# Two transformer layers on one core: four PSUM pairs in the V, K and Q stage, V's low parts dealt out otherwise, h's range in the third head, the last output half in another bank

## Chip, core and metric

One NeuronCore of a Trainium2 chip. The metric is the device time of one execution in microseconds (us). The five engines are named as in the profile: PE (TensorE, matrix products), DVE (VectorE), ACT (ScalarE), POOL (GpSimd) and SP (SyncE, which here only issues DMAs). PSUM, into which PE writes, has eight banks of 128 x 512 fp32; a "pair" is two neighbouring banks, 128 x 1024.

## What is computed

DEPTH is 2: layer 0 is multi-head latent attention, layer 1 differential attention, over 1024 latent tokens and 256 context tokens, width 1024. Cut to what matters here:

```python
for i in range(DEPTH):
    shift, scale, gate = adaln(c, ada_w[i], ada_b[i])          # also for the context
    h = x * (1 + scale) + shift;  h_c = ctx * (1 + scale_c) + shift_c
    if i == 0: o, o_c = mla_mixer(h, h_c, ...)                 # 16 heads, 96-wide q and k, 64-wide v
    else:      o, o_c = diff_mixer(h, h_c, ...)                # 8 heads, two softmaxes each
    x = layer_norm(ALPHA * x + gate * (o @ out_w[i]), ln_g[i], ln_b[i])
    # context the same, in layer 0 only
# mla_mixer: q from a 256-wide and k, v from a 128-wide latent; o = softmax(q k^T * s) v, times silu(gate)
```

## The kernel before, in words

Every fp32 operand is held as a high and a low part, and a product takes three matmuls (`mm3`, L185 to L187). The program runs in stages: projections of layer 0; a short stage that makes V for all heads and K and Q of head 0 (L873 to L884); the 16 heads of layer 0; its output projection (L1146 to L1180); layer 1.

PE's order is written out by hand in all stages that matter here (`manual_schedule`, engine P; in the V, K and Q stage DVE's order too, in the output projection all four engines'). Elsewhere a planner orders DVE, ACT, POOL and SP, and it also chooses, among the buffers of a tag, the one that comes free first. Every engine runs its own instructions in order.

**V, K and Q stage.** Five generators are stepped through in a fixed list (L880). Each makes a product in a PSUM pair (`pair()`), and the pair comes free when its last reader is done. In PE's order, with names that the text below uses:

- P: the rotary part of q (12 matmuls of 512 columns); DVE shuffles and multiplies it (L290, L291), then L294 and L295 work on SBUF alone.
- K, Q: k and q of two heads; ACT writes the high part (stkH, stqH, L181), DVE the low part (stkL, stqL, L182). Kc, Pc, Qc are the same for the context, 256 columns.
- V0 to V9: V of a tile of 128 tokens, all heads (6 matmuls). ACT writes the high part Vh (L650). The low part Vl goes one of two ways: on DVE (L656), one instruction that reads the pair; or ACT copies the pair into a buffer `op` (L653) and POOL subtracts (L654). `op` has one buffer, so a second ACT copy waits until POOL has read the first.
- M0 to M3, MC: row maxima of head 0's first 512 queries: scores (L757, L763), DVE's maximum (L759, L764, L765), a turn on PE (L768) and a write into a row of qH (L769). The first true scores wait for it. M0 reads q and k that went through DMAs (L86) from the staging tiles, KH among them.

**A head** has 11 units; a unit makes scores for 256 keys (L833 to L835), ACT's exponential (L777) and rounding (L778), POOL's low part (L779), and two units later the products with V (L845 to L848). S0 is head 0's first unit. Between the units stand the row maxima for later queries and, in head 0 only, `h1_range` (L544 to L565): 4 small matmuls (L552) and 16 small DVE instructions that bound the size of the next layer's input. Its results are read only in layer 1.

**Output projection.** For each of 8 tiles two halves, y0 in a bank of tag `a` and y1 in the only bank of tag `b`. Behind tile 7 all eight banks become tag `b`, one is taken and left unused (L1181), and the first product of layer 1 (its K) takes another.

```python
    set_banks(a=3, d=2)                 # 613: three pairs, and two banks for the heads' results
            if t % 2 == 0:              # 651: which tiles of V go by ACT and POOL
            y1, y0 = bank("b"), bank("a")   # 1146
        bank("b")                       # 1181
```

## Time and profile before

| | |
|---|---|
| three runs | 1799.22, 1794.52, 1797.15 us; median 1797.15 |
| the profiled execution's own time | 1797.62 us |
| its span in the trace | 1795.8 us (1.8 us lie outside it) |
| mean granted PE clock | 0.988 of full speed |
| PE, DVE, ACT, POOL busy | 93%, 69%, 62%, 44% of the span |
| V, K and Q stage | 221.2 to 257.6 us in the span |
| heads 0 to 15 | 257.6 us to about 767 us |
| output projection of layer 0, with the changed tile 7 | to 905 us |

How rows are read: in a timeline a row has start, duration (us), engine, line of the kernel, operation, output<-inputs, shapes, number of instructions, and in brackets the engine's idle time before it and what ended that. A row of PE lists a matmul's whole passage; two matmuls overlap, so the pace is the distance of the starts. A row of the stretches has the length, then each engine's busy time and, behind "PEclk", the granted clock.

### The profile page before, as it was taken

How to read it: one execution, taken by the hardware profiler on the slowest of the kernel's cores; microseconds unless marked ns; L12 is line 12 of the kernel's file. 1: busy time of each engine (PE TensorE's matmuls, PEld its weight loads, DVE VectorE, ACT ScalarE, POOL GpSimd, SP SyncE). 2: the span in 40 equal slices, each digit the busy share in tenths (PEclk: the TensorE clock that was granted, in tenths of full speed). 3: DMA queues.
4: the chain of work that ended last, by engine and by line, in shares of the span. 5: the costliest groups of instructions: out<-in, count | busy, mean ns of one | idle time of the engine just before them, and what ended most of it. 6: DMA issues, size and time to landing. Idle time of an engine off the chain costs nothing. (4 is left out here: it accounts for less than half of the span.)

```text
span 1795.8 us, 36757 instructions
## 1 busy us (share of the span) xinstructions
PE 1668.3 (93%) x14564; PEld 1237.5 (69%) x14564; DVE 1236.9 (69%) x2047; ACT 1117.9 (62%) x2233; POOL 796.3 (44%) x722
## 2 busy tenths in 40 slices
PE   7999989999999998999999999989999999986998
PEld 7999955656666565577866666767676757574876
DVE  7658566566665757557746777787778777979564
ACT  3541167877777787835536676767675766666442
POOL 1422136767776676845541222222314131435454
PEclk9999999999999999999999999999999999998999
DMA  8258520110111112164432213121212122223331
GB/s 304 80 156 256 164 56 23 44 44 21 42 46 34 43 44 81 51 217 161 148 117 74 58 54 79 55 78 54 68 41 64 35 68 58 62 61 124 101 116 70
DMA packets 111225, 154.84 MB, mean 86 GB/s; under 512 B 13415, under 2 KB 84679, under 8 KB 111054
## 3 DMA queue, kind: packets, MB, share of 16 engines
q1 hardware_dynamic: 102654, 144.90, 27.3%
q10 hardware_dynamic: 8400, 7.61, 1.3%
q8 instruction: 114, 1.87, 0.4%
q14 instruction: 57, 0.47, 0.1%
HBM read 98.65 MB, written 27.07 MB: 70 GB/s over the span
## 5 line engine op out<-in xcount | busy, mean ns | idle before, releaser
L779 POOL TENSOR_TENSOR pl<-p,ph 128x1024 f16<-128x1024 f32 (+1 forms) x176 | 364.1, 2074 | 149.3 <-ACT ph L778 122.6
L1361 ACT ACTIVATE p<-ps_b,mx 128x512 f32<-128x512 f32 (+1 forms) x384 | 230.3, 617 | 89.0 <-DVE mx L1357 84.9
L777 ACT ACTIVATE p<-ps_a,esc 128x1024 f32<-128x1024 f32 (+1 forms) x176 | 189.0, 1074 | 93.4 <-PE ps_a L835 87.5
L759 DVE TENSOR_REDUCE mx<-ps_a 128x1 f32<-128x1024 f32 x128 | 155.2, 1222 | 127.7 <-PE ps_a L757 127.7
L778 ACT CAST ph<-p 128x1024 f16<-128x1024 f32 (+1 forms) x176 | 177.1, 1006 | 5.5
L1355 DVE TENSOR_REDUCE mx<-ps_b 128x1 f32<-128x512 f32 x256 | 165.3, 679 | 0.0
L848 PE MATMUL ps_d<-Vh,pl 128*128 128x65 f16 x1344 | 146.0, 194 | 4.5 <-POOL pl L779 4.4
L845 PE MATMUL ps_d<-Vh,ph 128*128 128x65 f16 x1344 | 148.2, 195 | 0.0
L847 PE MATMUL ps_d<-Vl,ph 128*128 128x64 f16 x1344 | 146.9, 193 | 0.0
L1386 POOL TENSOR_TENSOR sm<-sm,us 128x1 f32<-128x1 f32 x64 | 17.9, 280 | 273.6 <-DVE sm L1365 263.5
L1338 PE MATMUL ps_b<-KS,QS 128*128 128x512 f16 (+1 forms) x384 | 125.7, 345 | 12.9 <-DVE pl L182 7.1
L845 PEld LDWEIGHTS <-ph 128*128 128x128 f16 x1344 | 123.3, 97 | 18.0 <-issue 4.6
L847 PEld LDWEIGHTS <-ph 128*128 128x128 f16 x1344 | 123.9, 98 | 12.1
L833 PE MATMUL ps_a<-qH,KH 100*128 100x512 f16 x320 | 121.5, 380 | 8.5 <-ACT p L777 4.2
L1339 PE MATMUL ps_b<-KS,Q 128*128 128x512 f16 (+1 forms) x384 | 129.0, 345 | 0.0
L848 PEld LDWEIGHTS <-pl 128*128 128x128 f16 x1344 | 123.2, 97 | 5.8 <-POOL pl L779 5.8
L181 ACT ACTIVATE ph<-ps_b,lcf 128x512 f16<-128x512 f32 (+1 forms) x192 | 115.1, 647 | 19.3 <-PE ps_b L1374 19.3
L182 DVE SCALAR_TENSOR_TENSOR pl<-ps_b,lcf,ph 128x512 f16<-128x512 f32 (+1 forms) x192 | 117.1, 653 | 13.5 <-ACT ph L181 13.5
L1374 PE MATMUL ps_b<-idr,p 128*128 128x128 f32 x640 | 103.6, 278 | 22.8 <-ACT p L1361 14.7
L834 PE MATMUL ps_a<-qH,KL 96*128 96x512 f16 x320 | 121.3, 379 | 0.0
L835 PE MATMUL ps_a<-qL,KH 96*128 96x512 f16 x320 | 120.7, 377 | 0.0
L1384 PE MATMUL ps_b<-vh,pl 128*128 128x128 f16 x640 | 111.3, 220 | 5.3 <-DVE pl L182 5.3
(427 smaller groups left out, 5261.0 us busy)
## 6 DMA issues: line engine op xcount, KB each, us to landing
ws<-in_dw SPq DMA_DIRECT2D x28, 512.0 KB, 3.9
adw<-in_ada_w SPq DMA_DIRECT2D x24, 512.0 KB, 4.9
adaw<-in_ada_w SPq DMA_DIRECT2D x16, 512.0 KB, 7.4
g<-sg_d SPq DMA_DIRECT2D x16, 512.0 KB, 7.3
sg_d<-gg ACTq DMA_DIRECT2D x40, 128.0 KB, 3.7
o_d<-op SPq DMA_DIRECT2D x7, 640.0 KB, 3.9
xt<-in_xT SPq DMA_DIRECT2D x16, 256.0 KB, 4.4
wgs<-in_w_in SPq DMA_DIRECT2D x32, 128.0 KB, 3.3
```

The source lines that it names most:

```text
L759: dve.tensor_reduce(mx[:, t, 0:1], ps, axis=AX.X, op=ALU.max)
L777: act.activation(p32[:, :n], st, AF.Exp, scale=esc0)
L778: act.copy(ph[:, :n], p32[:, :n])
L779: pool.tensor_tensor(pl[:, :n], p32[:, :n], ph[:, :n], op=ALU.subtract)
L833: pe.matmul(s_, kh[:nr, ks], QH[:nr, :], start=True, stop=False)
L845: pe.matmul(pv[:, t, :], ph[:, ts], Vh[:, k, h, :], start=(k == kcs[0] and t == 0), stop=False, skip_group_check=True)
L847: pe.matmul(pv[:, t, :V0], ph[:, ts], Vl[:, k, h, :], start=False, stop=False, skip_group_check=True)
L848: pe.matmul(pv[:, t, :], pl[:, ts], Vh[:, k, h, :], start=False, stop=(k == NT - 1), skip_group_check=True)
L1338: pe.matmul(out, qs[m][:, ts], ks[m][:, c0:c0 + n], start=True, stop=False)
L1339: pe.matmul(out, q1[m][:, ts], ks[m][:, c0:c0 + n], start=False, stop=True)
L1355: dve.tensor_reduce(mx[:, 2 + 2 * m + i:3 + 2 * m + i], b, axis=AX.X, op=ALU.max, negate=True)
L1361: act.activation(p[m][:, c0:c0 + n], b, AF.Exp, bias=nb, accum_out=sm[:, 2 + 3 * m + i:3 + 3 * m + i])
```

## The change

1. The V, K and Q stage gets four pairs instead of three and two single banks; the cut into three pairs and two banks follows behind it.
2. V0, V2, V4, V6 and V9 get their low parts on DVE; V1, V3, V5, V7 and V8 by ACT and POOL (before: the odd tiles on DVE, the even ones by ACT and POOL).
3. MC moves ahead of V7.
4. `ab1_of` and `h1_range` are asked for in head 2 instead of head 0.
5. y1 of tile 7 goes to the bank of tag `e`, and no bank is taken unused before layer 1's first product.

```diff
@@ -610 @@
-    set_banks(a=3, d=2)
+    set_banks(a=4)
@@ -648 prod_v0 @@
-            if t % 2 == 0:
+            if t in (1, 3, 5, 7, 8):
@@ -879 @@
         for g in (pq, pk, pq, vg, pq, pq, vg, pk, pk, pq, pq1, vg, pq2, pq2, pq2, vg,
-                  pm, vg, pm, vg, pm, vg, pm, vg, pm, vg, pm, vg):
+                  pm, vg, pm, vg, pm, vg, pm, pm, vg, vg, pm, vg):
             next(g)
+    set_banks(a=3, d=2)
@@ -948 @@
-            if h == 0:
+            if h == 2:
                 ab1_of()
-            hr = [(h1_range(pair), (0, 1, 0, 1, 1))] if h == 0 else []
+            hr = [(h1_range(pair), (0, 1, 0, 1, 1))] if h == 2 else []
@@ -1143 @@
-            y1, y0 = bank("b"), bank("a")
+            y1, y0 = bank("b" if t < 7 else "e"), bank("a")
@@ -1178 @@
         set_banks(b=8)
-        bank("b")
```

What the built programs show of the order. DVE in the V, K and Q stage, before, from P's last two steps on (the number behind a tile's name is its buffer; ps_a_2599 is Q's pair, ps_a_2616 V1's):

```order
L294 TENSOR_TENSOR rsw_2536<-rsw_2536,cs_2549 128x1024
L295 TENSOR_TENSOR rr_2537<-rr_2537,rsw_2536 128x1024
L182 SCALAR_TENSOR_TENSOR stqL_2541<-ps_a_2599,qsc_70,stqH_2540 128x1024
L182 SCALAR_TENSOR_TENSOR stpL_2543<-rr_2537,qsc_70,stpH_2542 128x1024
L656 SCALAR_TENSOR_TENSOR Vl<-ps_a_2616,vsc_68,Vh 128x1024
L182 SCALAR_TENSOR_TENSOR stkL_2539<-ps_a_2625,ksc_69,stkH_2538 128x256
```

The same place now (ps_a_2589 is V0's pair, ps_a_2598 Q's, ps_a_2643 V2's):

```order
L295 TENSOR_TENSOR rr_2537<-rr_2537,rsw_2536 128x1024
L656 SCALAR_TENSOR_TENSOR Vl<-ps_a_2589,vsc_68,Vh 128x1024
L182 SCALAR_TENSOR_TENSOR stqL_2541<-ps_a_2598,qsc_70,stqH_2540 128x1024
L182 SCALAR_TENSOR_TENSOR stpL_2543<-rr_2537,qsc_70,stpH_2542 128x1024
L182 SCALAR_TENSOR_TENSOR stkL_2539<-ps_a_2625,ksc_69,stkH_2538 128x256
L656 SCALAR_TENSOR_TENSOR Vl<-ps_a_2643,vsc_68,Vh 128x1024
```

The low part of V0 now stands on DVE ahead of Q's, and that of V1 has left it.

ACT at the end of the stage, now, from V6's high part to head 0's first exponential (ps_a_2737 is V7's pair, ps_a_2748 V8's, ps_a_2762 V9's):

```order
L650 ACTIVATE Vh<-ps_a_2717,vsc_68 128x16x64
L650 ACTIVATE Vh<-ps_a_2737,vsc_68 128x16x64
L653 ACTIVATE op_2745<-ps_a_2737,vsc_68 128x1024
L650 ACTIVATE Vh<-ps_a_2748,vsc_68 128x16x64
L653 ACTIVATE op_2756<-ps_a_2748,vsc_68 128x1024
L650 ACTIVATE Vh<-ps_a_2762,vsc_68 128x16x64
L777 ACTIVATE p_341_2548<-ps_a_2778,esc_71 128x1024
```

Before, the copies into `op` were V6's and V8's, with V7's high part alone between them; now those of V7 and V8 follow each other.

DVE in head 2 now, at the maxima of its second half of queries:

```order
L553 TENSOR_REDUCE hm<-ps_a_3937 128x2
L764 TENSOR_REDUCE mx_3794<-ps_a_3944 128x4
L555 TENSOR_SCALAR hm<-hm 128x1
L769 SCALAR_TENSOR_TENSOR qcH_3676<-ps_a_3963,sh_72,selt_64 2x256
L556 TENSOR_TENSOR hm<-hm 128x1
L557 SCALAR_TENSOR_TENSOR hm<-hm 128x1
L765 TENSOR_REDUCE ng_3795<-mx_3794 128x4
L300 TENSOR_SCALAR hm<-hm 128x1
L301 RECIPROCAL hm<-hm 128x1
L303 TENSOR_SCALAR hun<-hm 128x1
L302 TENSOR_SCALAR hsc<-hm 128x1
L560 TENSOR_TENSOR hm<-hm,hsc 128x1
```

These rows, and six more up to L769's write into qH, stood at the same place of head 0 before, row for row; in head 0 now only L764, L769, L765 and L769 are left there. The instructions of `ab1_of` and the first reductions of `h1_range` (L538 to L547) have not moved on DVE: the planner puts them into the stage before V, K and Q in both programs.

## The prediction

> **What bounds the kernel now.** I read the totals first, then PE's waits in the changed stage, then the stretches, then the rows behind each wait.

> ```profile
> PE 1668.3 (93%) x14564; PEld 1237.5 (69%) x14564; DVE 1236.9 (69%) x2047; ACT 1117.9 (62%) x2233; POOL 796.3 (44%) x722
> ```

> PE is busy for 93% of the span. So in most stages nothing but PE's own pace counts, and time can only be won where PE stands idle or runs at a low clock. PE's waits from 221 us to 258 us, the V, K and Q stage (matrix product and what it waited for: us in total, times, longest):

> ```profile
> PE ps_a L768 <- DVE ng L765: 2.1, 1, 2.1
> PE ps_a L185 <- DVE stqL L182: 2.0, 1, 2.0
> PE ps_a L757 <- DVE Vl L656: 1.3, 2, 0.7
> PE ps_a L185 <- DVE mx L759: 1.1, 2, 0.5
> PE ps_a L185 <- DVE Vl L656: 0.6, 1, 0.6
> ```

> That is 7.1 us of waiting, all of it for DVE. The stretches (length, then busy us of PE, PEld, DVE, ACT, POOL, the granted clock, DMA share, GB/s) show a second loss:

> ```profile
> 221.20:257.60 36.40, 29.23 (x121) 21.08 (x120) 23.23 (x22) 21.50 (x23) 11.68 (x7) 0.91 0.30 80
> 234.80:241.60 6.80, 6.17 (x21) 4.55 (x20) 2.42 (x4) 3.14 (x6) 2.06 (x1) 0.50 0.38 92
> ```

> From 234.80 to 241.60 PE ran at half clock. Its 6.17 busy us there would be 3.1 at full clock, so the spell costs 3.1 us. No engine fills the stage: the fullest behind PE, DVE, is busy for 23.23 of 36.40 us. It is bound by hand-overs, that is by which reader releases which pair.

> **The change part by part.** All sums are made against the profiled execution, 1797.62 us, 0.47 us above the median of the three runs, 1797.15.

> **Term 1, the stage.** The rows of the first long wait, from the timeline (start, duration):

> ```profile
> 227.95 1.22 DVE L294 TENSOR_TENSOR rsw<-rsw,cs 128x1024 f32<-128x1024 f32 x1
> ...
> 229.10 2.07 POOL L654 TENSOR_TENSOR Vl<-op,Vh 128x1024 f16<-128x1024 f32 x1 [5.58 <-ACT op L653]
> 229.20 3.06 DVE L295 TENSOR_TENSOR rr<-rr,rsw 128x1024 f32<-128x1024 f32 x1
> ...
> 232.18 1.27 DVE L182 SCALAR_TENSOR_TENSOR stqL<-ps_a,qsc,stqH 128x1024 f16<-128x1024 f32 x1
> ...
> 233.51 0.50 PE L185 MATMUL ps_a<-wvH,latH 128*128 128x512 f32 x1 [2.04 <-DVE stqL L182]
> ```

> L295 has the shape of L294, yet it takes 3.06 us instead of 1.22, and it does so while POOL's 2.07 us instruction runs beside it. Now V0's low part is DVE's, so POOL has nothing at that point. I take L294's 1.22 for L295 (the other end is 3.06, if POOL wasn't the cause), so it ends at 230.4 instead of 232.2. V0's low part (1.28) follows, to 231.65. With four pairs V2 uses V0's pair, no longer Q's, and starts at 231.7 instead of 233.51. [...]

> For the rest of the stage I need the pace of PE and of the readers. Two starts on PE, the readers' groups (times, busy, mean ns) and one transfer:

> ```profile
> 223.99 0.39 PE L185 MATMUL ps_a<-latH,wkH 128*128 128x512 f32 x1
> ...
> 225.35 0.39 PE L185 MATMUL ps_a<-wvH,latH 128*128 128x512 f32 x1
> ```

> ```profile
> L654 POOL TENSOR_TENSOR Vl<-op,Vh 128x1024 f16<-128x1024 f32 x5 | 10.3, 2068 | 24.4 <-ACT op L653 24.4
> L650 ACT ACTIVATE Vh<-ps_a,vsc 128x1024 f16<-128x1024 f32 x9 | 10.0, 1114 | 7.8 <-PE ps_a L187 7.8
> ...
> L653 ACT ACTIVATE op<-ps_a,vsc 128x1024 f32<-128x1024 f32 x5 | 5.5, 1107 | 0.0
> L656 DVE SCALAR_TENSOR_TENSOR Vl<-ps_a,vsc,Vh 128x1024 f16<-128x1024 f32 x4 | 5.1, 1281 | 5.9 <-ACT Vh L650 5.9
> L759 DVE TENSOR_REDUCE mx<-ps_a 128x1 f32<-128x1024 f32 x4 | 4.7, 1213 | 0.0
> ```

> ```profile
> KH<-stkH SPq DMA_DIRECT2D x16, 160.0 KB, 2.6
> ```

> Six matmuls of 512 columns take 225.35 - 223.99 = 1.36 us; six of 256 half of that, 0.7; a maximum's two score products a third, 0.45. The new order, walked with these and 0.05 to 0.15 us for each hand-over:

> - V2 runs 231.7 to 233.1. Pc takes V1's pair, which ACT frees: Q's high part to 230.9, V1's to 232.1, P's to 233.2, the copy into `op` to 234.2. Pc starts at 234.25 (before 236.01), and Qc and V3 follow to 237.05.
> - M0 needs Kc's part of KH. ACT writes it by 234.65, and 2.6 us later it has landed: M0 at 237.5. This is the new wait where the pairs no longer stop PE: 0.45 us.
> - M0 to M3, MC and V4 to V8 are 5 x 0.45 + 5 x 1.36 = 9.05 us of PE. Waits of 0.4 (V6 for V4's low part), 0.1 (V7 for M2's maximum) and 0.3 (V8 for V6's low part) are left: V8 ends at 247.4.
> - DVE then ends M3's maximum, L764 and L765 at 248.5; L768 at 248.65; V9 1.36; S0 at 250.05.

> The same places before, PE's and ACT's:

> ```profile
> 254.53 1.22 DVE L764 TENSOR_REDUCE mx<-ps_a 128x4 f32<-128x1024 f32 x1
> ...
> 256.08 0.22 PE L768 MATMUL ps_a<-idr,ng 128*4 128x128 f32 x1 [2.12 <-DVE ng L765]
> ...
> 257.58 0.39 PE L833 MATMUL ps_a<-qH,KH 100*128 100x512 f16 x1
> ...
> 259.10 1.11 ACT L777 ACTIVATE p<-ps_a,esc 128x1024 f32<-128x1024 f32 x1 [0.20 <-PE ps_a L835]
> ...
> 261.76 1.11 ACT L777 ACTIVATE p<-ps_a,esc 128x1024 f32<-128x1024 f32 x1 [0.47 <-PE ps_a L835]
> ```

> S0 comes 257.58 - 250.05 = 7.5 us earlier: 4.4 of waits that shrink and 3.1 for the spell, which I take as gone, since the wait of 2.04 us just before it is gone. Not all of that lasts. `op` has one buffer, and V7's and V8's copies now stand next to each other: POOL works on V7's from 248.2 to 250.25, V8's copy waits for that and ends at 251.4, V9's high part at 252.45, and only then comes the first exponential: 6.65 before 259.10. It keeps ACT busy until the second (1.11, then L778's rounding of 1.05) at 254.7, which is 7.06 before 261.76. From there PE leads again. **Term 1: -7.1 us.** Bounds: with L295 at 3.06 the first 1.8 us go; if V8's copy hides, 0.5 to 1.0 more is won; KH landing late costs up to 1.2; the spell's return 3.1.

> **Term 2, `h1_range` out of head 0, and term 3, into head 2.** The same stretch (fourth unit's scores to the sixth's) in head 2, then in head 0:

> ```profile
> 330.56:335.65 5.09, 4.96 (x72) 3.21 (x69) 4.01 (x6) 3.82 (x4) 3.73 (x3) 1.00 0.32 103
> 265.82:274.05 8.23, 5.41 (x76) 3.80 (x73) 7.41 (x21) 5.12 (x5) 5.95 (x4) 1.00 0.09 24
> ```

> With `h1_range` the stretch takes 3.14 us more, though its matmuls are 5.41 - 4.96 = 0.45. The rest lies here:

> ```profile
> 269.65 2.12 POOL L779 TENSOR_TENSOR pl<-p,ph 128x1024 f16<-128x1024 f32 x1 [0.83 <-ACT ph L778]
> ...
> 270.03 1.76 DVE L556 TENSOR_TENSOR hm<-hm 128x1 f32<-128x1 f32 x1
> ...
> 272.08 0.22 PE L768 MATMUL ps_a<-idr,ng 128*4 128x128 f32 x1 [1.44 <-DVE hm L300]
> ...
> 334.45 2.13 POOL L779 TENSOR_TENSOR pl<-p,ph 128x1024 f16<-128x1024 f32 x1 [0.77 <-ACT ph L778]
> ```

> L556 has one column, yet it takes 1.76 us, until POOL's L779 ends; L765 stands behind it, PE's L768 waits 1.44 for that, and the next scores behind qH's row wait 1.4 more. The rows in the order of the program stand in head 2 just as they stood in head 0, and L779 starts there at the same distance from the unit (3.89 us behind the fourth unit's scores in head 2, 3.83 in head 0). So I take the collision over whole: -3.14 and +3.14, **sum 0**. Bounds of the sum: -3.1, if head 2 covers it all, to +3.1, if the two gaps bring a half-clock spell.

> **Term 4, the last output half.** PE, DVE and ACT there:

> ```profile
> 904.71 0.68 DVE L1083 TENSOR_TENSOR z<-ps_b,gate 128x512 f32<-128x512 f32 x1
> ...
> 905.44 0.38 PE L185 MATMUL ps_b<-h1H,wx 128*128 128x512 f16 x1 [2.00 <-DVE z L1083]
> ...
> 908.40 1.24 ACT L1092 ACTIVATE z<-z,mv 128x1024 f32<-128x1024 f32 x1 [5.88 <-POOL mv L1091]
> ...
> 910.62 0.60 PE L1103 MATMUL ps_b<-idr,z 128*128 128x128 f32 x4
> ```

> Layer 1's K no longer waits 2.00 us for L1083 to read the bank. But behind K stands L1103, which needs ACT's L1092, and that ends at 909.64 whatever K does. K ends at about 908.4, and PE waits until about 909.9 instead of 910.62. **-0.7 us** (bounds 0 and -2.0).

> Sum: -7.1 + 0 - 0.7 = -7.8. **1797.62 - 7.8 = 1789.8 us.** My forecast's own range is 1787.5 to 1792.

> **The rivals.**

> *B: a half-clock spell stays or comes back.* The stretches of the same length behind the waits of 2.12 us (before 256.08) and 2.00 us (before 905.44):

> ```profile
> 256.00:262.80 6.80, 5.52 (x25) 2.85 (x26) 3.77 (x4) 4.44 (x5) 3.50 (x2) 1.00 0.01 2
> 905.40:912.20 6.80, 6.76 (x39) 3.89 (x39) 2.82 (x4) 3.27 (x6) 2.22 (x4) 1.00 0.38 133
> ```

> The clock is 1.00 in both, while the half clock of 234.80 to 241.60 follows the wait of 2.04 us, so the wait alone doesn't decide. New waits could meet it: Pc's and L768's of 1.2 us, or head 2's pair of 1.4. Price 3.1 us: 1789.8 + 3.1 = 1792.9. [...]

> *C: the change doesn't do what it says.* Other readers take the place of DVE's: the single `op`, ACT's 21.50 busy us in a stage of 29, or a slow L295. Speaks for it: ACT would be at 74%, and the stage was bound by hand-overs before. If half of the 7.1 waits' gain of 4.4 and the spell's 3.1 fail, term 1 is -2 to -4: 1793.5 to 1796.

> *D: slower.* In head 2 the two gaps of term 3 (1.44 and 1.4 us within 3.4) close the clock, and it stays at half. The nearest row is a stretch of layer 1:

> ```profile
> 1647.00:1665.00 18.00, 10.06 (x40) 7.91 (x41) 15.47 (x19) 7.79 (x20) 12.61 (x8) 0.53 0.30 87
> ```

> There it stayed for 18 us. A head has no such slack (4.96 of 5.09 us busy), so each us at half clock costs 0.5. 13 us are needed to be visibly slower, hence a spell of 26 us: 1789.8 + 13 = 1803. Against it: PE idles for 8 of the 18 us there, and in a head at half clock it wouldn't.

> **How the numbers follow.** Forecast 0.66, B 0.17, C 0.10, D 0.07. The measurement tells 0.3% (5.4 us) from no change: faster below 1791.8, slower above 1802.5. The forecast's range lies nearly whole below 1791.8, and I move 0.04 of it to "same": faster 0.62; same 0.04 + 0.17 + 0.10 = 0.31; slower 0.07. The range leaves out D, C's upper end and the sums in which head 2 covers the whole collision: 1787 to 1796.

> **What would show each step.** Term 1: L295 at 1.2 us, V2's start at 231.7, the granted clock at 1.00 throughout the stage, S0 at 250 and the second exponential at 254.7; a wait of ACT's L653 for POOL of about 1 us. Term 2: head 0's fourth to sixth unit in 5.1 us; term 3: head 2's in 8.2, with L556 at 1.8. Term 4: K's start at about 896.2 (903.3 - 7.1), and L1103 waiting for ACT's L1092. The forecast is wrong if a low clock shows between 221 and 350 us, if L295 stays at 3 us, or if the sixth unit of head 2 doesn't come about 3 us late.

## The result, and the profile after

| | before | changed |
|---|---|---|
| median of 20 executions | 1798.46 us (1794.52 to 1802.60) | 1794.38 us (1788.10 to 1798.00) |
| mean of the same | 1798.50 us | 1793.38 us |
| the profiled execution | 1797.62 us | 1789.83 us |

The ratio is 0.9971 with a 95% interval of 0.9963 to 0.9979: the change gains 3.8 to 6.6 us. The forecast was 1789.8 us (range 1787 to 1796). The single profiled execution lies on it to 0.03 us. The median lies 4.6 us above it, inside the range, but outside the 1787.5 to 1792 that the sum's own bounds gave; the part of the range that holds it had been left open for the rivals. So there are two questions: whether each step happened as worked out, and why the mean gain of 5.1 us is smaller than the 7.8 us between the two profiles.

The totals and PE's waits in the V, K and Q stage, as they were shown of before:

```profile
PE 1665.7 (93%) x14564; PEld 1235.5 (69%) x14564; DVE 1235.6 (69%) x2047; ACT 1116.9 (62%) x2233; POOL 796.2 (45%) x722
```

```profile
PE ps_a L768 <- DVE ng L765: 0.9, 1, 0.9
PE ps_a L185 <- DVE Vl L656: 0.9, 3, 0.4
PE ps_a L763 <- DVE mx L759: 0.9, 1, 0.9
PE ps_a L185 <- ACT op L653: 0.9, 1, 0.9
PE ps_a L757 <- DMA KH<-stkH: 0.5, 1, 0.5
PE ps_a L833 <- ACT p L777: 0.3, 1, 0.3
```

The list reaches into head 0 (L763 and L833 are behind the stage). Inside the stage 3.2 us of waiting are left of 7.1, none is over 0.9, and two of them have a new releaser: ACT's copy into `op`, and the transfer of KH. The stretches: the stage from P's start to S0, then head 0's fourth to sixth unit, then head 2's:

```profile
220.70:250.07 29.37, 26.20 (x120) 19.14 (x118) 21.50 (x22) 20.23 (x23) 10.36 (x6) 1.00 0.37 100
258.17:263.26 5.09, 4.97 (x73) 3.22 (x70) 4.00 (x6) 3.76 (x4) 3.73 (x3) 1.00 0.00 0
319.77:328.07 8.30, 5.41 (x76) 3.81 (x73) 7.48 (x21) 5.18 (x5) 6.08 (x4) 1.00 0.30 86
```

The stage takes 29.37 us instead of 36.34 (257.58 - 221.24), at the full clock. Head 0's stretch fell to 5.09, head 2's rose to 8.30. The timeline of the stage, in the order of the walk in the prediction (P starts at 220.70 here, 0.54 us earlier than before, which nothing in the change explains: the work ahead of it is the same, and over all 14 profiles P starts between 219.91 and 223.19):

```profile
228.67 1.23 DVE L295 TENSOR_TENSOR rr<-rr,rsw 128x1024 f32<-128x1024 f32 x1
...
231.14 0.50 PE L185 MATMUL ps_a<-wvH,latH 128*128 128x512 f32 x1 [0.38 <-DVE Vl L656]
...
233.66 0.38 PE L185 MATMUL ps_a<-latH,wqH 128*128 128x256 f32 x1 [0.85 <-ACT op L653]
...
237.28 0.59 PE L757 MATMUL ps_a<-KH,qH 96*128 96x512 f16 x2 [0.53 <-DMA KH<-stkH]
...
248.50 0.22 PE L768 MATMUL ps_a<-idr,ng 128*4 128x128 f32 x1 [0.90 <-DVE ng L765]
...
250.01 1.11 ACT L653 ACTIVATE op<-ps_a,vsc 128x1024 f32<-128x1024 f32 x1 [1.17 <-POOL Vl L654]
250.07 0.39 PE L833 MATMUL ps_a<-qH,KH 100*128 100x512 f16 x1
...
252.02 1.12 ACT L777 ACTIVATE p<-ps_a,esc 128x1024 f32<-128x1024 f32 x1
...
254.12 1.11 ACT L777 ACTIVATE p<-ps_a,esc 128x1024 f32<-128x1024 f32 x1
```

L295 takes 1.23 us, and the copy for V8 waits 1.17 us for POOL. The collision in head 2, and then the last output half (all lines behind the stage's list are one higher than in before, so L1104 is the old L1103):

```profile
323.66 2.12 POOL L779 TENSOR_TENSOR pl<-p,ph 128x1024 f16<-128x1024 f32 x1 [0.76 <-ACT ph L778]
...
323.99 1.81 DVE L556 TENSOR_TENSOR hm<-hm 128x1 f32<-128x1 f32 x1
...
326.09 0.22 PE L768 MATMUL ps_a<-idr,ng 128*4 128x128 f32 x1 [1.50 <-DVE hm L300]
```

```profile
895.24 0.39 PE L187 MATMUL ps_e<-oH,tL 128*128 128x512 f32 x1
895.47 0.39 PE L185 MATMUL ps_b<-h1H,wx 128*128 128x512 f16 x1
...
900.58 1.24 ACT L1093 ACTIVATE z<-z,mv 128x1024 f32<-128x1024 f32 x1 [5.87 <-POOL mv L1092]
...
901.88 1.09 PE L1104 MATMUL ps_b<-idr,z 128*128 128x128 f32 x8 [1.05 <-ACT z L1093]
```

K follows the last product at once, and 1.05 us of the 2.00 come back as a wait for ACT's z. From the last product to the turn it is 901.88 - 895.24 = 6.64 us instead of 910.62 - 903.04 = 7.58. Whether that 0.94 us reaches the end is another question, which e3_tail answers below.

### The profile page after: what moved, and what is told of

It reads as the page before. It is cut to its first block, busy times and chain, and to the rows that moved or that the text cites. A ratio compares the mean times of both kernels' runs of the same rounds, so it can differ in the third digit from the quotient of the medians.

```text
span 1788.0 us, 36754 instructions
## 1 busy us (share of the span) xinstructions
PE 1665.7 (93%) x14564; PEld 1235.5 (69%) x14564; DVE 1235.6 (69%) x2047; ACT 1116.9 (62%) x2233; POOL 796.2 (45%) x722
## 5 line engine op out<-in xcount | busy, mean ns | idle before, releaser
L779 POOL TENSOR_TENSOR pl<-p,ph 128x1024 f16<-128x1024 f32 (+1 forms) x176 | 364.3, 2075 | 146.5 <-ACT ph L778 120.6
L777 ACT ACTIVATE p<-ps_a,esc 128x1024 f32<-128x1024 f32 (+1 forms) x176 | 189.1, 1074 | 93.0 <-PE ps_a L835 86.9
L759 DVE TENSOR_REDUCE mx<-ps_a 128x1 f32<-128x1024 f32 x128 | 155.2, 1222 | 127.8 <-PE ps_a L757 127.7
L778 ACT CAST ph<-p 128x1024 f16<-128x1024 f32 (+1 forms) x176 | 177.1, 1006 | 5.5
L833 PE MATMUL ps_a<-qH,KH 100*128 100x512 f16 x320 | 121.5, 380 | 7.5 <-ACT p L777 3.1
L182 DVE SCALAR_TENSOR_TENSOR pl<-ps_b,lcf,ph 128x512 f16<-128x512 f32 (+1 forms) x192 | 117.1, 654 | 14.2 <-ACT ph L181 14.1
L835 PE MATMUL ps_a<-qL,KH 96*128 96x512 f16 x320 | 120.7, 377 | 0.0
```

The source lines that it names most:

```text
L759: dve.tensor_reduce(mx[:, t, 0:1], ps, axis=AX.X, op=ALU.max)
L777: act.activation(p32[:, :n], st, AF.Exp, scale=esc0)
L778: act.copy(ph[:, :n], p32[:, :n])
L779: pool.tensor_tensor(pl[:, :n], p32[:, :n], ph[:, :n], op=ALU.subtract)
L833: pe.matmul(s_, kh[:nr, ks], QH[:nr, :], start=True, stop=False)
```

## The experiments

Three numbers of each trace tell most, since they leave out what lies before: the second exponential counted from P's start (the stage), the last exponential of head 15 counted from the second one (the heads), and the turn of tile 7 counted from the output projection's last product (the tail). Half clock is given where it falls into them.

| kernel | stage | heads | tail | half clock there |
|---|---|---|---|---|
| before | 40.52 | 504.86 | 7.58 | stage, 6.8 us |
| changed | 33.42 | 504.98 | 6.64 | none |
| e1_stage | 33.45 | 505.27 | 7.57 | none |
| e2_range | 38.11 | 507.11 | 7.58 | head 2, 3.4 us |
| e3_tail | 40.52 | 504.90 | 6.64 | stage, 6.8 us |
| e5_pairs | 41.75 | 505.40 | 7.58 | stage, 3.4 us; its end and head 0, 10.2 us |
| e6_deal | 40.30 | 509.05 | 9.26 | stage to head 0, 3.4, 3.4 and 6.8 us; head 14, 3.4; tail, 3.4 |
| e7_order | 33.23 | 507.55 | 6.64 | head 2 and head 14, 3.4 us each |
| e8_best | 33.41 | 506.50 | 6.64 | head 2, 3.4 us |
| e9_late | 33.85 | 502.91 | 6.63 | none |
| e10_late_op | 33.08 | 502.88 | 6.64 | none |
| e11_again | 33.79 | 504.94 | 6.66 | none |
| e12_head4 | 33.31 | 502.43 | 6.66 | none |

### One part at a time

**e1_stage** undoes parts 4 and 5:

```diff
-            if h == 2:
+            if h == 0:
                 ab1_of()
-            hr = [(h1_range(pair), (0, 1, 0, 1, 1))] if h == 2 else []
+            hr = [(h1_range(pair), (0, 1, 0, 1, 1))] if h == 0 else []
...
-            y1, y0 = bank("b" if t < 7 else "e"), bank("a")
+            y1, y0 = bank("b"), bank("a")
...
         set_banks(b=8)
+        bank("b")
```

> Only parts 1 to 3 of the change (four pairs, the deal of V's low parts, MC ahead of V7); h's range stays in head 0, the last output half in its old bank. Theory A (the half-clock spell of 3.1 us belongs to the long wait, whatever the execution): 7.1 us faster than before, in the mean of the executions too. Theory B (the spell comes in some executions only, by the phase of the clock's windows, so the profile of before counts it too high): 4.5 to 6 us faster in the mean, while a single profile can differ from that of before by more. Theory C (the loss against the forecast lies in head 2): 7 to 8 us faster.

Measured: median 1793.82 us (12 runs) against 1798.53 (29 runs), ratio 0.9978 (0.9967 to 0.9990), that is 1.8 to 5.9 us faster. The stage took 33.45 us, as in the changed kernel. Theory C falls: without head 2 the gain isn't larger. Theory A's 7.1 us lies outside the interval; of theory B's 4.5 to 6 us the interval holds nearly all, though the means differ by only 4.0 us. The windows that theory B names show in the profile of before: half clock (0.50) lasts 3.41 us from 26.57, 6.83 from 234.78 and 17.06 from 1647.90, one, two and five times 3.41.

**e2_range** makes part 4 alone:

```diff
-            if h == 0:
+            if h == 2:
                 ab1_of()
-            hr = [(h1_range(pair), (0, 1, 0, 1, 1))] if h == 0 else []
+            hr = [(h1_range(pair), (0, 1, 0, 1, 1))] if h == 2 else []
```

> Only part 4: h's range in head 2 instead of head 0; the stage and the tail as before. Theories A and B: no change, within 1.4 us of before; in the profile head 0's fourth to sixth unit takes 5.1 us and head 2's 8.2. Theory C: 2 to 3 us slower. The profile is also a second look at the old V, K and Q stage: by A a half-clock spell of 6.8 us stands there again, by B it may be missing.

Measured: ratio 0.9992 (0.9981 to 1.0002), no change that can be told. The profile is worth more. Its V, K and Q stage is that of before, instruction for instruction. The stage's stretch and the long wait in it:

```profile
221.16:255.09 33.93, 26.45 (x121) 19.06 (x119) 23.23 (x22) 21.39 (x23) 11.65 (x7) 1.00 0.32 86
```

```profile
233.42 0.50 PE L185 MATMUL ps_a<-wvH,latH 128*128 128x512 f32 x1 [2.04 <-DVE stqL L182]
```

The wait is 2.04 us, as in before, and yet the clock stays at 1.00 and the stage takes 33.93 us instead of 36.34. This time head 2 has a spell behind its two gaps:

```profile
334.00:337.30 3.30, 3.30 (x31) 2.00 (x29) 1.15 (x1) 1.91 (x2) 0.00 (x0) 0.50 0.00 0
```

**e3_tail** makes part 5 alone:

```diff
-            y1, y0 = bank("b"), bank("a")
+            y1, y0 = bank("b" if t < 7 else "e"), bank("a")
...
         set_banks(b=8)
-        bank("b")
```

> Only part 5: the last output half in the bank of tag e. All theories: 0.7 to 2 us faster, K at once behind the output projection's last product and a wait of about 1 us of L1103 for ACT's z. The profile is a third look at the old V, K and Q stage: by A the half-clock spell stands there, by B it may be missing.

Measured: ratio 1.0000 (0.9987 to 1.0014): the gain that was expected can't be told from none. In the trace the tail is 0.94 us shorter (6.64 instead of 7.58). But 55 us behind the turn PE waits for ACT at layer 1's first scores, and ACT waits there for a transfer. ACT's row and PE's, of before, then of e3_tail (whose lines are one lower behind the output projection):

```profile
957.59 1.06 ACT L992 ACTIVATE wsq<-ws 128x1024 f32<-128x1024 f32 x1 [5.99 <-DMA ws<-in_dw]
...
964.92 0.38 PE L1338 MATMUL ps_b<-KS,QS 128*128 128x512 f16 x1 [2.10 <-ACT p L1361]
```

```profile
958.47 1.06 ACT L992 ACTIVATE wsq<-ws 128x1024 f32<-128x1024 f32 x1 [7.22 <-DMA ws<-in_dw]
...
965.80 0.38 PE L1337 MATMUL ps_b<-KS,QS 128*128 128x512 f16 x1 [3.33 <-ACT p L1360]
```

Counted from the last product, these scores start at 61.88 us in before and at 62.23 in e3_tail; over the four profiles with the old tail and no spell in it the mean is 61.8 (60.9 to 62.3), over the eight with the new tail 62.0 (61.4 to 62.7). So the 0.94 us have turned into a longer wait at that place, and from the last product to the end of the span the two groups take 890.0 and 890.2 us. PE's wait lasts until that transfer; why it and the one ahead of it (`in_ada_w`, issued 0.9 us earlier with the new tail) land no earlier isn't shown. The old stage again has its spell:

```profile
222.41:258.75 36.34, 29.19 (x120) 21.04 (x119) 23.23 (x22) 21.50 (x23) 11.65 (x7) 0.91 0.29 80
236.10:242.90 6.80, 6.25 (x23) 4.64 (x21) 2.30 (x4) 3.25 (x5) 2.06 (x1) 0.51 0.38 89
```

So the same old stage is 36.34 us with the spell in two profiles, and 33.93 without it in one.

### When a wait brings the half clock

**e4_gaps** is the kernel before with a row of waits of known length behind its end:

```diff
+    set_banks(g=1)
+    with tc.manual_schedule(engines={ET.PE, ET.DVE}):
+        for k in range(168):
+            y = bank("g")
+            for _ in range(30 + 7 * k % 12):
+                pe.matmul(y, idr, oHL[NOW][0][:, :512], start=True, stop=True)
+            for n in (...)[k % 7]:
+                dve.tensor_reduce(hm[:, 0:1], y[:, :n], axis=AX.X, op=ALU.max)
```

> The kernel before, and behind its end 168 groups of 30 to 41 matmuls of 512 columns into one bank, each group waiting for DVE's reductions of that bank: waits of seven lengths, from 1.4 to 3 us, 24 of each. The output is that of the kernel before. Theory A: all waits of 2.0 us and more are followed by half clock, none of 1.5 us. Theory B: of the waits of 2 us a part, some 3 to 5 in 10, those that lie wholly in one window of about 3.4 us; the share grows with the wait's length.

Three of the groups (PE's rows: the wait ahead of each in brackets), and three stretches of one window's length:

```profile
1811.94 7.74 PE L1610 MATMUL ps_g<-o,idr 128*128 128x512 f32 x32 [1.90 <-DVE hm L1612]
1821.72 9.37 PE L1610 MATMUL ps_g<-o,idr 128*128 128x512 f32 x39 [2.03 <-DVE hm L1612]
1833.25 9.73 PE L1610 MATMUL ps_g<-o,idr 128*128 128x512 f32 x34 [2.17 <-DVE hm L1612]
```

```profile
1834.04:1837.45 3.41, 3.41 (x10) 2.62 (x9) 0.00 (x0) 0.00 (x0) 0.00 (x0) 0.50 0.00 0
1820.39:1823.80 3.41, 2.08 (x9) 1.73 (x10) 1.20 (x3) 0.00 (x0) 0.00 (x0) 1.00 0.00 0
1823.80:1827.21 3.41, 3.41 (x17) 2.73 (x16) 0.00 (x0) 0.00 (x0) 0.00 (x0) 1.00 0.00 0
```

Behind the wait of 2.17 us PE runs at half clock from 1834.04 to 1837.45. Count windows of 3.4133 us (1894.4 us between two starts of half clock in this trace, divided by 555; in before 730.45 us from the start at 234.78 to the one at 965.23, divided by 214) back from 1834.04: the window ahead is 1830.63 to 1834.04, and the whole wait (1831.08 to 1833.25) lies in it. The wait of 2.03 us (1819.69 to 1821.72) is cut by the border at 1820.39, so only 1.33 us of it fall into one window, and the next window has the full clock. Counted over all waits of the trace:

| wait, us | 1.5 | 1.9 | 2.0 | 2.2 | 2.5 | 2.7 | 3.0 |
|---|---|---|---|---|---|---|---|
| followed by half clock | 0 of 24 | 5 of 24 | 11 of 24 | 14 of 24 | 18 of 24 | 20 of 24 | 20 of 23 |

Sorted by the larger part that falls into one window of this grid, instead of by length, almost nothing is left to chance in this trace: of 77 waits with less than 1.85 us in a window none is followed by half clock, of 79 with over 1.95 us all are (of the 11 between, 9). Theory B holds, and theory A falls. How long the spells lasted goes with the same grid. Counted over all 14 profiles from 100 us on, a half-clock window in which PE stood idle for less than 0.5 us was followed by full clock (169 of 169), one with more than 0.7 us by another at half clock (61 of 61), and of the 10 between 6. In before PE stood idle for 0.63 us of the window that began at 234.78, and the spell there had two windows. In the profile of before the same grid fits the two waits that brought no spell: from the spell's start at 234.80 the borders fall at 255.28 (6 windows on) and at 903.8 (196 on), inside the waits that end at 256.08 and 905.44, so that 1.32 us of the one and 1.64 of the other are the most that lie in one window. In e4's own copy of the kernel before the windows lie otherwise: there is half clock in the stage for one window behind the wait of V2 and for one behind L768's wait of 2.12 us (from 253.69), and there is one at the tail:

```profile
905.70:909.00 3.30, 3.30 (x9) 1.10 (x9) 1.51 (x3) 0.40 (x1) 1.01 (x3) 0.50 0.68 219
```

There the turn came 9.25 us behind the last product instead of 7.58: that window cost 1.67 us there.

### Which part of the stage's change does it

**e5_pairs** takes the four pairs alone, **e6_deal** the deal of the low parts (with MC ahead of V7) alone:

```diff
# e5_pairs, against before
-    set_banks(a=3, d=2)
+    set_banks(a=4)
...
             next(g)
+    set_banks(a=3, d=2)
# e6_deal, against before
-            if t % 2 == 0:
+            if t in (1, 3, 5, 7, 8):
...
-                  pm, vg, pm, vg, pm, vg, pm, vg, pm, vg, pm, vg):
+                  pm, vg, pm, vg, pm, vg, pm, pm, vg, vg, pm, vg):
```

> Only the four pairs; V's low parts and MC as before. L295 then still runs beside POOL's low part of V0 and takes 3.06 us, but V2 no longer waits for Q's low part behind it. If the number of pairs is what the stage lacked: V2 starts within 0.5 us of Kc's end and the stage is 3 to 4 us shorter than that of before, beside a spell. If the deal of V's low parts is what counts: V2 still waits 1.5 us or more and the stage gains under 2 us.

> Only the new deal of V's low parts and MC ahead of V7; three pairs as before. L295 has no POOL beside it and takes 1.2 us. If the pairs are what the stage lacked: V2 still waits for Q's low part, which now stands behind V0's, and starts at most 0.6 us earlier than in before. If the deal counts most: V2 starts 1.8 us earlier.

Measured: e5_pairs 1799.97 us against 1797.58, ratio 1.0014 (1.0002 to 1.0027); e6_deal 1804.19, ratio 1.0032 (1.0018 to 1.0045). Each half alone is slower than before, which neither theory had. With pairs alone V2 doesn't wait any more, but L295 still takes 3.05 us beside POOL:

```profile
228.63 2.06 POOL L654 TENSOR_TENSOR Vl<-op,Vh 128x1024 f16<-128x1024 f32 x1 [5.59 <-ACT op L653]
228.73 3.05 DVE L295 TENSOR_TENSOR rr<-rr,rsw 128x1024 f32<-128x1024 f32 x1
```

And PE waits at the end of the stage instead:

```profile
PE ps_a L833 <- DVE Vl L656: 2.5, 1, 2.5
PE ps_a L768 <- DVE ng L765: 2.1, 1, 2.1
```

S0 waits there for V9's low part (253.83 to 256.35). Half clock begins at 252.35, behind the wait for L765, and with S0's wait in it it lasts for three windows, 10.2 us. With the deal alone POOL has nothing beside L295:

```profile
228.68 1.23 DVE L295 TENSOR_TENSOR rr<-rr,rsw 128x1024 f32<-128x1024 f32 x1
```

V2 starts 0.6 us earlier from P's start on (232.35 - 220.72 against 233.51 - 221.24), as the first theory said. But PE now waits elsewhere in the stage (1.64 us in one piece, for a low part of V on DVE), half clock comes five times up to the tail, and this stands at the start of the output projection, 500 us later:

```profile
PE ps_a L185 <- ACT hb L1107: 3.0, 1, 3.0
```

In the built program the heads hand on their three pairs in another turn, and it ends so that the first tile's first product gets a bank of the pair that ACT's L1107 is still reading. In the changed kernel PE waits 0.7 us at that place, for DVE. How the profile's extra time divides between these waits and the spells is not worked out here.

### Taking `h1_range` off the path

**e7_order** steps `h1_range` behind the maxima in head 2, and **e8_best** gives V8's copy another buffer on top:

```diff
# e7_order, against the changed kernel
-            run_step(units0(h, 0), hr + [(max0(h, 1), (1, 1, 2, 1, 1)), ...
+            run_step(units0(h, 0), [(max0(h, 1), (1, 1, 2, 1, 1)), ...
-                                    (kq, ...)] + low[0])
+                                    (kq, ...)] + hr + low[0])
# e8_best, on top
-                vf = w0("op").rearrange(...)[:, :1024].rearrange(...)
+                vf = (w0("p32") if t == 8 else w0("op").rearrange(...)[:, :1024]).rearrange(...)
```

> The changed kernel with h's range stepped behind the row maxima in head 2 instead of ahead of them, so that L765 no longer stands behind L556. If the collision of L556 with POOL's L779 is what makes that stretch 3.1 us longer: fourth to sixth unit of head 2 in 5.4 to 5.8 us instead of 8.2, and 2.4 to 2.8 us off the mean beside fewer spells there. If the four small matmuls and the sixteen DVE instructions themselves cost it: no change.

> As e7_order, and V8's copy goes to one of the idle exponential buffers instead of the single op buffer, so that ACT needn't wait for POOL. If that wait of 1.17 us holds up the first exponential on the path: the first exponential 1.1 us earlier and 0.7 to 1.1 us off beyond e7_order. If PE has other work meanwhile: under 0.3 us.

Measured: e7_order 1790.83 us, ratio 0.9960 (0.9946 to 0.9974); e8_best 1790.73, 0.9958 (0.9942 to 0.9974); the two can't be told apart, nor can they from the changed kernel's 0.9971 and, in its second measurement below, 0.9961. The stretch fell only to 7.84 in e7_order, not to 5.8. L765 was free, but now the write into qH stands behind `h1_range`, and PE waits for that one in a single piece. DVE's row and PE's:

```profile
323.85 1.60 DVE L556 TENSOR_TENSOR hm<-hm 128x1 f32<-128x1 f32 x1
...
327.26 0.38 PE L833 MATMUL ps_a<-qH,KH 100*128 100x512 f16 x1 [1.92 <-DVE qH L769]
```

A half-clock window followed, and another in head 14 behind a wait of 1.7 us for ACT (the heads' 507.55 holds both). So the collision is the reason, as expected, but the order had only moved it from one row maximum's step to the next. In e8_best ACT's wait for POOL is gone, and M0 waits 1.0 us for KH instead of 0.5: nothing is left of it at the second exponential (33.41; 33.08 in e10_late_op, where M0 waits 0.6).

**e9_late** steps `h1_range` at the end of head 2's second half, and **e10_late_op** adds e8's buffer:

```diff
-            hr = [(h1_range(pair), (0, 1, 0, 1, 1))] if h == 2 else []
-            run_step(units0(h, 0), hr + [(max0(h, 1), ...
+            hr = [(h1_range(pair), (0, 0, 0, 0, 0, 3))] if h == 2 else []
+            run_step(units0(h, 0), [(max0(h, 1), ...
...
-                                                   (qs, ...)] + low[1])
+                                                   (qs, ...)] + low[1] + hr)
```

> The changed kernel with h's range stepped at the end of head 2's second half, behind that half's last row maxima, where no score waits for DVE. If the stretch of 8.2 us is long only because the row in qH stands behind h's range on DVE: fourth to sixth unit of head 2 in 5.1 us, a second half no longer than before, 3 us less than the changed kernel in a profile without a half-clock spell, 2.5 to 4 us less in the mean. If the instructions find other work to hold up there: 1 us or less.

> As e9_late, and V8's copy in an idle exponential buffer, as in e8_best. By what e8_best's profile showed (ACT's wait gone, but PE's wait for KH longer by 0.5 us): 0 to 0.5 us less than e9_late.

Measured: e9_late 1789.71 us, ratio 0.9953 (0.9941 to 0.9965); e10_late_op 1792.15, 0.9961 (0.9948 to 0.9974), not to be told from each other, nor from the changed kernel measured beside them (e11_again, 0.9961). In e9_late head 2's stretch falls to 5.09 us, as expected, and the heads are 2.07 us shorter (502.91 against 504.98), where 3 had been expected. The whole profiled span is not shorter (1790.0 us, against 1788.0 and 1790.0 in the changed kernel's two profiles). The wait of e6_deal is back at the start of the output projection, and 6.8 us of half clock (from 788.70) stand at the same place:

```profile
PE ps_a L185 <- ACT hb L1108: 3.0, 1, 3.0
```

**e11_again** is the changed kernel once more; no edit.

> The changed kernel, unchanged, for more executions and a second profile. If what the clock's windows do by chance is all that lies between the 7.8 us of the two first profiles and the 4 to 5 us of the medians: stage from P's start to the second exponential again 33.2 to 33.5 us, turn of tile 7 again 6.6 us behind the last product, and a mean 4.5 to 6.5 us under that of before, with half-clock spells at other places than in the first profile.

Measured: 1791.73 us (5 runs) against 1798.00, ratio 0.9961 (0.9948 to 0.9974). By the means that is 7.1 us less than before (interval 4.7 to 9.4), more than the 4.5 to 6.5 that were expected and than the first measurement's 5.1, though the two intervals overlap. Stage 33.79, a little above what was expected, since M0 waits 0.89 us for k's low part (KL) instead of 0.53 for KH; tail 6.66; no half clock from 31 us to 958 us.

**e12_head4** is e9_late with `h == 4` for `h == 2` in both places:

> As e9_late, but in head 4 instead of head 2: the pairs behind the heads then fall as in the changed kernel (tile 0's second half no longer gets the bank that L1108 still reads). If e9_late's gain in the heads was lost to that bank: heads 2.4 us shorter than in the changed kernel, no wait of 3.0 us for L1108 at the start of the output projection, 2 to 3 us less in the mean than the changed kernel, some 8 us less than before. If the wait has another cause: 3 us of waiting there again, and no gain.

Measured: **1787.18 us (6 runs, 1786.25 to 1789.15) against 1798.03, ratio 0.9941 (0.9928 to 0.9953)**, the lowest ratio of all. The heads take 502.43 us, 2.55 less than in the changed kernel, and at the start of the output projection PE waits only the old 0.7:

```profile
PE ps_a L185 <- DVE tL L177: 0.7, 1, 0.7
```

So e9's gain in the heads had been lost to the bank behind them, as its theory said: from the heads' last exponential to the output projection's last product it takes 140.33 us in e9_late and 135.97 here (136.14 in the changed kernel). Of these 4.4 us the wait is 2.3; the rest I put down to the half clock beside it, which nothing here separates.

## Why the prediction was right, and where it was off

**The walk through the stage was right.** From P's start: V2 at 10.46 predicted and 10.44 measured, Pc 13.01 and 12.96, M0 16.26 and 16.58 (it waits for KH, as said), S0 28.81 and 29.37, the second exponential 33.46 and 33.42. ACT's copy for V8 waits 1.17 us for POOL where about 1 us was forecast. What the first step rests on is shown: L295 takes 3.05 us with POOL's L654 beside it (e5_pairs) and 1.23 without (e6_deal, and the changed kernel); why the two hold each other up is not. That the four pairs and the new deal gain nothing without each other was not foreseen.

**The step that failed is the size of the spell in term 1**: "3.1 for the spell, which I take as gone, since the wait of 2.04 us just before it is gone". It is gone, but it was not in every execution of before. With it the stage to the second exponential is 40.52 us (before, e3_tail; 40.46 in e4's copy, with two single windows), without it 38.11 (e2_range). So it costs 2.4 us, not 3.1: PE's busy time in the stage is 2.7 us longer with it (29.19 against 26.45 us), and 0.3 of that fills waits. And e4_gaps shows a wait of 2.0 us bringing half clock in 11 of 24 cases. In the mean the stage's waits are then worth 38.11 - 33.42 = 4.7 us, and the spell some 1.1 (2.4 x 11/24, an estimate) where the sum had 3.1. I had read one execution as the kernel's state; its profile carried a spell that not every execution has.

**Terms 2 and 3 were right**: the heads take 504.86 us before and 504.98 now. The stretch costs 3.21 us in head 2 (8.30 - 5.09), as 3.14 before in head 0, with the same collision.

**Term 4's wait was right, its gain was not.** The turn comes 0.94 us earlier behind the last product, where 0.7 was worked out. But the sum carries this to the end, and it is lost 55 us later, where PE waits for ACT and ACT for a transfer that doesn't move (e3_tail): a wait further on that the prediction didn't look for. In the sum term 4 is about 0, not -0.7.

**The sum in the mean.** It is then 4.7 us without any spell and 5.8 with this one. The measured 3.8 to 6.6 us and, the second time, 4.7 to 9.4 hold both; so does e1_stage, without term 4, with 1.8 to 5.9. What this leaves out is that the other waits that went, L768's 2.12 us and the tail's 2.00, brought spells in some executions too (e4's copy has both). How often all these come in the executions that were timed isn't settled by these numbers.

**The two profiles differ by the forecast's 7.8 us partly by luck.** Up to the turn of tile 7: 0.54 us lie ahead of the stage, 7.10 in it, -0.12 in the heads, 0.28 in the output projection and 0.94 in the tail, together 8.74 (910.62 - 901.88); 1.0 is lost again behind it, 0.7 of it up to layer 1's first scores.

**The rivals.** The median of 1794.38 us lies nearer to B's 1792.9 than to the forecast. B named the right thing, that the wait alone doesn't decide, but the spell did not stay (none of the eight profiles with the whole new stage has one in it): what decided in e4_gaps is how a wait lies in the clock's windows of 3.41 us, with half clock behind all 79 waits that had over 1.95 us in one window. C was seen in part: `op` and KH do hold PE up, for 0.9 and 0.5 us, but both are in the walk's sum. (C's time leaves term 4 out: with its own -2 to -4 and the -0.7 it is 1792.9 to 1794.9, not 1793.5 to 1796.) D didn't come: the half clock behind head 2's gaps lasted 3.4 us where it came (e2_range, e7_order, e8_best), not 26; PE was busy in nearly all of that window (for 3.30 of 3.30 us in e2_range's row), and the next one was at full clock.

**What stays open.** The spells that the stage lost should show as a higher mean clock. Measured side by side, they do once and don't once: 0.9894 (5 of e11_again) against 0.9879 (11 of before), but 0.9880 (12 of e1_stage) against 0.9887 (29 of before). Whether others came in their place more often, or whether so few executions can't tell, these runs don't settle.

## What to carry to other kernels

A profile is one execution: before a stretch at half clock is counted as a gain, look whether it stands there in a second profile, and count it by how often it comes. A shorter wait is a gain only if the next wait on the way moves with it: follow it to the end, here to a transfer 55 us on. To remove a wait in a ring of buffers, walk all readers of the ring: here more buffers alone and a new deal of the readers alone only moved the wait to the next hand-over (both were slower than before). And an instruction that nobody needs soon belongs where nobody stands behind it; then look far behind as well, for a change in head 2 turned the ring of pairs so that a 3 us wait stood at the output projection.

## What was unexpected of the hardware

A DVE instruction of one column (L556) took 1.76 us in before, 1.81 in the changed kernel and 1.60 in e7_order where POOL's L779 ran, and one of 1024 columns (L295) 3.05 in e5_pairs beside POOL's L654, instead of 1.23. In these rows it didn't end before POOL's was done: L556 ended within 0.02 us of L779's end (before and changed), L295 1.1 us behind L654's, which is nearly its own 1.23.
